# Two-layer encoder trunk: late rows squared behind evictions, roundings placed behind exponentials, memory keys and values loaded in place, the FFN's last unit in another order

## The chip, the cores and the metric

The kernel runs on one core of one Trainium2 chip. The time is the device time of one execution in microseconds. The core's engines are PE (TensorE, matrix products; its weight loads are shown as PEld), DVE (VectorE), ACT (ScalarE), POOL (GpSimd) and SP (SyncE, which issues transfers). Each engine runs its instructions in order; engines wait for one another through semaphores.

## The reference

Two layers over 1024 tokens of width 1024. Layer 0 mixes tokens by windowed attention (16 heads, 4 key/value heads, rotary, a sink per head), layer 1 by a bidirectional gated recurrence (HGRN2). Each mixer also has four heads that attend to 256 memory tokens, and each layer ends in a gated channel mixer with a short convolution. Cut to what matters:

```python
for layer in range(DEPTH):
    u = rmsnorm(h, norm_g[layer, 0])
    mem_kv = mem_n @ w_mem_kv[layer]
    y = mixer_window_attn(u, mem_kv, ...) if layer == 0 else mixer_hgrn2(u, mem_kv, ...)
    h = h + rmsnorm(y, norm_g[layer, 1])
    f = conv_ffn(rmsnorm(h, norm_g[layer, 2]), ffn_w_in[layer], ffn_conv_w[layer], ...)
    h = h + rmsnorm(f, norm_g[layer, 3])

def mixer_window_attn(u, mem_kv, w_in, sink, w_out, pos):
    q, k, v, xq = jnp.split(u @ w_in, [...], axis=-1)
    q, k = rope(q, pos), rope(k, pos)
    o = window_gqa_sink(q, k, v, sink)
    return jnp.concatenate([o, memory_cross_attn(xq, mem_kv)], axis=-1) @ w_out

def conv_ffn(v, w_in, conv_w, conv_b, w_out):
    gate, up = jnp.split(v @ w_in, 2, axis=-1)
    return (jax.nn.gelu(dwconv_centred(gate, conv_w, conv_b)) * up) @ w_out
```

## The kernel before

An fp32 product is made of three products of rounded parts: each operand is split into a rounded part (`wh`, `uh`, ...: a cast, mostly on ACT) and the rest (`wl`, `ul`, ...: a subtraction, mostly on DVE), and `mm3` (L81 to L83) or `mmk` (L535) issues high by high, low by high and high by low. A scheduler places all instructions of the program on their engines by its own estimate of time; `tc.issue_after(ins)` makes it place what is inside behind `ins`. So the order of the work is that of the schedule, and a change of one line can move others.

The program: `start()` projects the memory tokens to keys and values for both layers, stores them in `kvd`, and brings in the input; `window()` is layer 0's mixer, `Out` its output projection, `ffn` its channel mixer; `hgrn()`, `Out` and `ffn` do the same for layer 1.

**The rows' norms in layer 0.** The input is projected without its norm. The reciprocal root of each row's mean square (`rs`) is applied later: `rooted` (L1272) makes it from the sum of squares `xss` (L1274 on DVE, L1275 on POOL) and scales cos and sin (L1277) and two more factors by it. The sums come from `square` in `start()`: a load of 128 rows of x on SP (L1336) into one of three buffers, and an ACT square with a running sum (L1337). There are eight; the last three (rows 5, 6 and 7) are called together.

**The first projection.** `proj(g)` makes queries, keys and values of head group g, token block by token block (eight blocks of 128). `token(t)` runs 24 matmuls into `pj` (two buffers), turns the queries and keys on DVE (L277, L278) and POOL (L279, L280), casts v on ACT (L282) and takes its rest on DVE (L283), which is the last reader of that `pj` buffer. `turn` transposes (`ptq`, L295) and splits again. The tiles `kh`, `kl` and `v` live in one pool for even groups and in another for odd ones.

**The cross heads.** For each of the four memory heads, `cross_head` (L182 to L187) loads its keys and values from `kvd` into a tile `kv` (L185), and splits them into `kvh` (ACT, L86) and `kvl` (DVE, L87), one buffer each. In layer 0 `kv` has a tile of its own in the pool `ea`; in layer 1 it takes one of the five `E` buffers of the recurrence, so its load waits until one is free.

**The output projection's operands.** The heads' outputs go to `oT` in memory and come back: `Out.read` (L428 to L430) loads six 128-row pieces into `ul`, casts them to `uh` on ACT (L429) and takes the rest on DVE (L430). Group 3's own outputs (pieces 6 and 7) are moved inside the core and cast in `attend` (L375, L376) right behind that transfer. `wo0.begin` (L456) reads eight column blocks in turn.

**The FFN.** Units f = 0 to 21 of hidden columns are computed with seven products each (k = 1 to 7) of sums and differences of halves. Products 6, 7 and 4 use the bank X, 5 and 3 use V, 2 uses Y. ACT copies X to `su`, `g` (two halves) and V to `s5`; DVE adds; `conv` makes the gate.

## Time and profile before

| | us |
|---|---|
| median of three runs | 2674.11 |
| the three runs | 2675.33, 2672.37, 2674.11 |
| the profiled execution's own time | 2671.58 |
| its span, first to last instruction | 2669.8 |
| DVE busy | 1822.3 |
| ACT busy | 1379.6 |
| POOL busy | 471.4 |

The span is one execution's and is 1.8 us shorter than that execution's time. A timeline row has the start, the duration, the engine, the line, the operation, output <- input, its shape, and in brackets how long its engine had idled before it and what ended that. PE's matmuls overlap, so their distance from start to start is the cost of one, not the duration. The mean granted clock of PE over the span is 0.996 of full speed.

### The profile page before, as it was taken

To read this page: it belongs to the slowest core of one execution; us is meant where nothing else is said; L and a number is where in the kernel's file an instruction comes from. 1 tells how busy PE (TensorE), PEld (TensorE's weight loads), DVE (VectorE), ACT (ScalarE), POOL (GpSimd) and SP (SyncE) were. 2 spreads that over 40 slices of the span, in tenths; PEclk is the share of its full clock that TensorE was granted. 3 is DMA by queue.
4 is the path that set the end of the run, shared out by engine and by line. 5 is a ranking of instruction groups with operands and counts; after the bars stand their busy time and mean duration, and the time that the engine had idled before them with its cause. 6 is when DMAs were issued, how large, how long until landed. Compare 5 with 4: busy or idle time off the path is not lost.

```text
span 2669.8 us, 39096 instructions
## 1 busy us (share of the span) xinstructions
PE 2606.9 (98%) x14420; PEld 2188.4 (82%) x14420; DVE 1822.3 (68%) x3043; ACT 1379.6 (52%) x2503; POOL 471.4 (18%) x519
## 2 busy tenths in 40 slices
PE   8999999999999999999999999999999999999998
PEld 7888887788888887887887888888888788888887
DVE  6688786578555565478688686886757755656447
ACT  6467677445444445455454554645534444444453
POOL 0331120211111100031224131230311111110013
PEclk9999999999999999999999999999999999999999
DMA  9682223367777857574235352113436778785666
GB/s 369 222 181 59 70 69 95 104 193 193 199 201 193 210 145 259 193 246 151 87 108 147 84 123 60 48 29 92 143 126 177 188 199 210 197 204 161 223 190 236
DMA packets 195728, 425.93 MB, mean 160 GB/s; under 512 B 20048, under 2 KB 56272, under 8 KB 189904
## 3 DMA queue, kind: packets, MB, share of 16 engines
q1 hardware_dynamic: 161840, 325.11, 37.8%
q0 software_dynamic: 24544, 90.19, 16.3%
q10 hardware_dynamic: 9152, 8.14, 1.0%
q8 instruction: 113, 1.85, 0.3%
q14 instruction: 79, 0.65, 0.1%
HBM read 330.04 MB, written 116.39 MB: 167 GB/s over the span
## 4 chain that ended last, share of the span: by engine, by line
PE 78%; DVE 12%; DMA 4%; ACT 3%; issue 2%; POOL 1%; SPq 0%; ACTq 0%; DVEq 0%; POOLq 0%
PE X L535 27%; PE V L535 11%; PE pj L81 6%; PE pj L82 5%; PE pj L83 5%; PE Y L535 5%; PE pb L81 4%; PE pb L82 4%; PE pb L83 4%; DVE E L1091 1%; PE pt L362 1%; DVE ER L1126 1%; PE po L1194 1%; DVE wl L87 1%; DVE EP L1127 1%
## 5 line engine op out<-in xcount | busy, mean ns | idle before, releaser
L87 DVE TENSOR_TENSOR wl<-st,wh 128x1024 fp32r<-128x1024 f32 (+1 forms) x238 | 263.7, 1114 | 326.5 <-ACT wh L86 308.8
L86 ACT CAST wh<-st 128x1024 fp32r<-128x1024 f32 (+1 forms) x238 | 222.5, 937 | 296.4 <-PE X L535 196.3
L81 PE MATMUL pj<-uh,wh 128*128 128x512 f32 x512 | 203.9, 399 | 5.9 <-DVE q L1036 2.7
L535 PE MATMUL X<-wl,wh 128*128 128x512 f32 x528 | 204.8, 390 | 0.2 <-DVE wl L87 0.2
L535 PE MATMUL X<-wh,wl 128*128 128x512 f32 x528 | 204.6, 389 | 0.0
L81 PE MATMUL pj<-wh,uh 128*128 128x384 f32 (+1 forms) x512 | 191.5, 375 | 11.9 <-DVE v L283 6.6
L82 PE MATMUL pj<-ul,wh 128*128 128x512 f32 x512 | 202.3, 396 | 0.1
L83 PE MATMUL pj<-uh,wl 128*128 128x512 f32 x512 | 202.0, 395 | 0.0
L535 PE MATMUL X<-wh 128*128 128x512 f32 x528 | 198.7, 390 | 1.0 <-ACT c L908 1.0
L83 PE MATMUL pj<-wh,ul 128*128 128x384 f32 (+1 forms) x512 | 187.9, 368 | 0.0
L82 PE MATMUL pj<-wl,uh 128*128 128x384 f32 (+1 forms) x512 | 187.8, 367 | 0.1
L77 DVE TENSOR_TENSOR wl<-st,wh 128x1024 fp32r<-128x1024 f32 (+1 forms) x92 | 117.4, 1280 | 26.0 <-ACT wh L76 25.2
L535 PE MATMUL V<-uh,wh 128*128 128x512 f32 x344 | 133.8, 389 | 0.0
L535 PE MATMUL V<-ul,wh 128*128 128x512 f32 x344 | 133.8, 389 | 0.0
L535 PE MATMUL V<-uh,wl 128*128 128x512 f32 x344 | 133.8, 389 | 0.0
L76 ACT CAST wh<-st 128x1024 fp32r<-128x1024 f32 (+1 forms) x98 | 98.8, 1014 | 39.7 <-PE pj L82 25.0
L81 PEld LDWEIGHTS pj<-uh,wh 128*128 128x128 f32 x512 | 96.5, 189 | 26.3 <-DVE q L1036 3.6
L535 PEld LDWEIGHTS X<-wh 128*128 128x128 f32 x528 | 99.1, 188 | 22.0 <-ACT c L908 1.4
L81 PEld LDWEIGHTS pj<-wh,uh 128*128 128x128 f32 x512 | 97.4, 190 | 23.7 <-issue 9.3
L535 PEld LDWEIGHTS X<-wl,wh 128*128 128x128 f32 x528 | 99.1, 188 | 21.3 <-DVE wl L87 0.8
L535 PEld LDWEIGHTS X<-wh,wl 128*128 128x128 f32 x528 | 99.1, 188 | 20.7
L83 PEld LDWEIGHTS pj<-uh,wl 128*128 128x128 f32 x512 | 96.7, 189 | 19.1
(390 smaller groups left out, 7169.5 us busy)
## 6 DMA issues: line engine op xcount, KB each, us to landing
st<-hid SPq DMA_DIRECT2D x154, 256.0 KB, 3.1
st<-in_ffw_dram SPq DMA_DIRECT2D x108, 256.0 KB, 2.9
w2s<-in_ffw_dram POOLq DMA_DIRECT2D x24, 1024.0 KB, 8.0
st<-in_ffw_dram SPq DMA_DIRECT2D x46, 512.0 KB, 4.4
hid<-tt SPq DMA_DIRECT2D x88, 256.0 KB, 4.8
st<-w2s SPq DMA_DIRECT2D x88, 256.0 KB, 3.4
sx<-in_ffw_dram SPq DMA_DIRECT2D x84, 256.0 KB, 3.9
sy<-in_ffw_dram SPq DMA_DIRECT2D x42, 512.0 KB, 6.2
```

Of the source, the lines that this page charges most:

```text
L76: act.copy(h[:, :n], raw)
L77: (eng or dve).tensor_tensor(l[:, :n], raw, h[:, :n].bitcast(F32), op=ALU.subtract)
L81: pe.matmul(o, ah, bh, start=first, stop=False)
L82: pe.matmul(o, ah, bl, start=False, stop=False)
L83: pe.matmul(o, al, bh, start=False, stop=last)
L86: act.copy(h, src)
L87: dve.tensor_tensor(l, src, h.bitcast(F32), op=ALU.subtract)
L362: pe.transpose(tp[:, j, :], sm[:, j, c * P:(c + 1) * P], ident)
L535: pe.matmul(o, x, y, start=new, stop=e, skip_group_check=not first)
L1091: dve.tensor_tensor_scan(B[:, rev], smask, a_[:, rev], 0.0, op0=ALU.mult, op1=ALU.add)
L1126: dve.tensor_tensor(re_, re_, bc(pl_[:, :, e:e + 1], [P, nb, n]), op=ALU.mult)
L1127: dve.tensor_tensor(pl_, pl_, bc(pe_[:, :, e:e + 1], [P, nb, n]), op=ALU.mult)
```

## The change

Four parts.

- The sums of squares of rows 5, 6 and 7 leave `start()`. In `proj(0)`, behind the v cast of tokens 0, 1 and 2, `token(t)` loads row block t + 5 into a tile `row` that has the memory of `kh`, `kl` and `v` of the odd groups, which are not in use yet, and squares it there.
- `cross_head` loads the keys and values straight into `kvl`, casts `kvh` from it and subtracts in place. The tile `kv` of layer 0 and the `E` buffer of layer 1 are no longer taken. The load now has to wait for the last reader of the previous head's `kvl`.
- The casts and subtractions of group 3's pieces 6 and 7 are made by `split_moved`, behind the exponentials of an even block that follows (the last right away), and the casts of `Out.read` for column blocks 6 and 7 are placed behind the exponentials of group 3's block 1.
- The last unit of each FFN has a body of its own, `last_unit`, with the products written in the order 6, 2, 7, 5, 4, 3; before: 2, 5, 6, 7, 3, 4.

```diff
@@ -179,9 +179,10 @@
                 nc.sync.dma_start(kvd[l][:, :, 1, t * P:(t + 1) * P].rearrange("h p d -> p h d"),
                                   vm[:, t, :].rearrange("p (h d) -> p h d", h=4))
 
-    def cross_head(l, h, wp, raw):
+    def cross_head(l, h, wp):
         kvh = wp.tile([P, 2, 256], F32R, tag="kvh", bufs=1, name="kvh")
         kvl = wp.tile([P, 2, 256], F32R, tag="kvl", bufs=1, name="kvl")
+        raw = kvl.bitcast(F32)
         nc.sync.dma_start(raw, kvd[l][h])
         split(kvh, kvl, raw)
         return *wunit(A["wxq"][l, h]), kvh, kvl
@@ -279,7 +280,14 @@
                 pool.tensor_tensor(rq[:, :320], t1, t2, op=ALU.add)
                 done = pool.tensor_tensor(rq[:, 320:], t1[:, 256:], t2[:, 256:], op=ALU.add)
                 sum_steps[0].send(done)
-                act.activation(v[:, t, :64], ps[:, 320:], AF.Copy, scale=rs0[:, t:t + 1])
+                cast = act.activation(v[:, t, :64], ps[:, 320:], AF.Copy, scale=rs0[:, t:t + 1])
+                if g == 0 and t + 5 < NT:
+                    tag = ("kh", "kl", "v")[t]
+                    row = ap_.tile([P, NT, P] if tag == "v" else [P, T], F32R, tag=tag, bufs=1, name="row").bitcast(F32)
+                    row = row.rearrange("p a b -> p (a b)") if tag == "v" else row
+                    nc.sync.dma_start(row, A["x"][(t + 5) * P:(t + 6) * P, :])
+                    with tc.issue_after(cast.ins):
+                        act.activation(row, row, AF.Square, accum_out=xss[:, t + 5:t + 6])
                 dve.scalar_tensor_tensor(v[:, t, 64:], ps[:, 320:], rs0[:, t:t + 1], v[:, t, :64].bitcast(F32),
                                          op0=ALU.mult, op1=ALU.subtract)
                 return rq
@@ -317,6 +325,14 @@
             return kept
 
         pairs, roped = {}, {}
+
+        marks, moved = {}, []
+
+        def split_moved():
+            ts_ = moved.pop()
+            oh, ol = uh[:, 6:8, ts_], ul[:, 6:8, ts_]
+            act.copy(oh, ol.bitcast(F32))
+            dve.tensor_tensor(ol, ol.bitcast(F32), oh.bitcast(F32), op=ALU.subtract)
 
         def attend(g, qkv, blocks=range(NT)):
             qs, kh, kl, v = qkv
@@ -346,8 +362,11 @@
                     dve.tensor_tensor(st["es"], sk[:, 4 * g:4 * g + 4], st["nm"], op=ALU.add)
                     act.activation(st["es"], st["es"], AF.Exp)
                     for j in range(4):
-                        act.activation(sm[:, j, :w], sm[:, j, :w], AF.Exp, bias=st["nm"][:, j:j + 1], scale=0.125,
-                                       accum_out=st["su"][:, j:j + 1])
+                        marks[g, n] = act.activation(sm[:, j, :w], sm[:, j, :w], AF.Exp, bias=st["nm"][:, j:j + 1],
+                                                     scale=0.125, accum_out=st["su"][:, j:j + 1])
+                    if moved and n % 2 == 0:
+                        with tc.issue_after(marks[g, n].ins):
+                            split_moved()
                     dve.tensor_tensor(st["su"], st["su"], st["es"], op=ALU.add)
                     dve.reciprocal(st["rd"], st["su"])
                     for j in range(4):
@@ -369,11 +388,11 @@
                     dve.tensor_tensor(ov, po[:64], ov, op=ALU.add)
                     if nn % 2 == 1 and g == 3:
                         ts_ = slice((n - 1) * P, (n + 1) * P)
-                        oh, ol = uh[:, 6:8, ts_], ul[:, 6:8, ts_]
+                        moved.append(ts_)
                         for hp in range(2):
                             nc.sync.dma_start(ul[hp * 64:(hp + 1) * 64, 6:8, ts_].bitcast(F32), o[:, hp::2, :])
-                        act.copy(oh, ol.bitcast(F32))
-                        dve.tensor_tensor(ol, ol.bitcast(F32), oh.bitcast(F32), op=ALU.subtract)
+                        if n == NT - 1:
+                            split_moved()
                     elif nn % 2 == 1:
                         ts_ = slice((n - 1) * P, (n + 1) * P)
                         for hp in range(2):
@@ -385,7 +404,7 @@
                 for _ in range(XU[g][b]):
                     xh_, xb_ = units.pop(0)
                     if xb_ == 0:
-                        xhead[0] = cross_head(0, xh_, ea, ea.tile([P, 2, 256], F32, tag="kv", bufs=1, name="kv"))
+                        xhead[0] = cross_head(0, xh_, ea)
                     cross_unit(0, xh_, xb_, xhead[0], ap_, tags, ea, pair)
 
         dve.tensor_scalar_mul(sk8, sk, 8.0)
@@ -398,7 +417,7 @@
         attend(3, cur)
         wo0.open()
         y0 = wo0.w1.tile([P, NT, 512], F32, bufs=1, name="y0")
-        wo0.begin(psq, ("pj", "pj", "ptq"), [y0[:, t, :] for t in range(NT)])
+        wo0.begin(psq, ("pj", "pj", "ptq"), [y0[:, t, :] for t in range(NT)], {6: marks[3, 1], 7: marks[3, 1]})
         psp.release()
         ap_.release()
 
@@ -422,11 +441,12 @@
                     self.us[b, u] = wunit(A[self.key][b, u], pl=pl if i >= RING else None)
             self.b = b
 
-        def read(self, ks, c0, c1, eng):
+        def read(self, ks, c0, c1, eng, behind=None):
             c = (slice(None), slice(ks[0], ks[-1] + 1), slice(c0, c1))
             raw = ul[c].bitcast(F32)
             eng.dma_start(raw, oT[self.l][ks[0]:ks[-1] + 1, :, c0:c1].rearrange("k p t -> p k t"))
-            act.copy(uh[c], raw)
+            with tc.issue_after(behind.ins) if behind else nullcontext():
+                act.copy(uh[c], raw)
             dve.tensor_tensor(ul[c], raw, uh[c].bitcast(F32), op=ALU.subtract)
 
         def kept(self, ps, t, ks, first, last):
@@ -447,7 +467,7 @@
                 c = slice((k % 2) * 512, (k % 2 + 1) * 512)
                 mm3(ps, oh[:, i, :], ol[:, i, :], wh[:, c], wl[:, c], first and i == 0, last and i == 3)
 
-        def begin(self, psb, tags, y0):
+        def begin(self, psb, tags, y0, behind={}):
             self.psb, self.y0 = psb, y0
             self.banks += [(psb, t, tags.count(t)) for t in tags]
             eng = (nc.sync, act)[self.l]
@@ -456,7 +476,7 @@
                     with tc.high_priority(AHEAD):
                         self.read(self.groups[0], t * P, (t + 1) * P, eng)
                 else:
-                    self.read(self.groups[0], t * P, (t + 1) * P, eng)
+                    self.read(self.groups[0], t * P, (t + 1) * P, eng, behind.get(t))
                 ps = self.bank()
                 self.kept(ps, t, self.groups[0], True, True)
                 act.copy(y0[t], ps)
@@ -687,6 +707,30 @@
             dve.tensor_tensor(t2[:, hi], t2[:, lo], c[:, oi], op=ALU.subtract)
             for k, x in ((5, t1[:, lo]), (7, t1[:, hi]), (6, t2[:, lo]), (4, t2[:, hi])):
                 nc.sync.dma_start(hd[k, p], x)
+
+        def last_unit(w, x, v, y, s1, ahead):
+            u = fp.tile([P, T], F32, tag="u", bufs=1, name="u")
+            su = fp.tile([P, 512], F32, tag="su", bufs=1, name="su")
+            s5 = fp.tile([P, 512], F32, tag="s5", bufs=1, name="s5")
+            g = gtile()
+            prod(6, w(6), x, False)
+            act.copy(su, x)
+            prod(2, w(2), y, True)
+            dve.tensor_tensor(u[:, ti], y, s1, op=ALU.add)
+            ahead()
+            prod(7, w(7), x, False)
+            act.copy(g[:, tj], x)
+            prod(5, w(5), v, True)
+            act.copy(s5, v)
+            dve.tensor_tensor(g[:, tj], g[:, tj], s5, op=ALU.add)
+            ahead()
+            prod(4, w(4), x, False)
+            act.copy(g[:, ti], x)
+            ahead()
+            prod(3, w(3), v, False)
+            dve.tensor_tensor(u[:, tj], v, su, op=ALU.add)
+            ahead()
+            hidden(NF - 1, conv(NF - 1, g, u))
 
         def first_units():
             X, s, ops = [], {}, []
@@ -770,6 +814,10 @@
                 x = X.pop()
                 v, y = (psx.tile([P, 512], F32, tag=t, name=t) for t in "VY")
                 w = lambda k: operand(ops, k)
+                if f == NF - 1:
+                    last_unit(w, x, v, y, s[1], ahead)
+                    yield
+                    return
                 prod(2, w(2), y, True)
                 u = fp.tile([P, T], F32, tag="u", bufs=1, name="u")
                 dve.tensor_tensor(u[:, ti], y, s[1], op=ALU.add)
@@ -1223,8 +1271,7 @@
                 xh_, xb_ = units.pop(0)
                 if xhead[1] != xh_:
                     xhead[1] = xh_
-                    raw = early.tile([P, 512], F32, tag="E", bufs=5, name="kv")
-                    xhead[0] = cross_head(1, xh_, wp, raw.rearrange("p (a b) -> p a b", a=2))
+                    xhead[0] = cross_head(1, xh_, wp)
                 cross_unit(1, xh_, xb_, xhead[0], wp, tags, wp, pair)
 
         def head(h, r):
@@ -1359,8 +1406,7 @@
 
         parts = iter([(), (), (memory_rstd,)] + [(lambda k=k: part(k),) for k in range(KT - 1)]
                      + [(lambda: part(KT - 1), lambda: square(A["x"], 0, xss))]
-                     + [(lambda t=t: square(A["x"], t, xss),) for t in (1, 2, 3, 4)]
-                     + [tuple(lambda t=t: square(A["x"], t, xss) for t in (5, 6, 7))])
+                     + [(lambda t=t: square(A["x"], t, xss),) for t in (1, 2, 3, 4)])
 
         def step():
             for f in next(parts, ()):
```

How the schedule's rows move, at three places. First ACT, where `start()` ends and the first projection begins; before:

```order
L76 CAST wh<-st 128x768
L1337 ACTIVATE x,xss<-x 128x1024 x4
L282 ACTIVATE v<-pj,rs_86 128x64
L86 CAST kvh<-kv 128x512
L282 ACTIVATE v<-pj,rs_86 128x64 x3
L303 CAST qs<-ptq 64x512
L282 ACTIVATE v<-pj,rs_86 128x64
L86 CAST kh<-ptq 128x512
L305 CAST qs<-ptq 64x512
L303 CAST qs<-ptq 64x512
L305 CAST qs<-ptq 64x512
L282 ACTIVATE v<-pj,rs_86 128x64 x2
```

and with the change:

```order
L76 CAST wh<-st 128x768
L1384 ACTIVATE x,xss<-x 128x1024
L283 ACTIVATE v<-pj,rs_86 128x64 x2
L290 ACTIVATE row,xss<-row 128x1024 x2
L86 CAST kvh<-kvl 128x512
L283 ACTIVATE v<-pj,rs_86 128x64
L290 ACTIVATE row,xss<-row 128x1024
L283 ACTIVATE v<-pj,rs_86 128x64 x2
L311 CAST qs<-ptq 64x512
L86 CAST kh<-ptq 128x512
L313 CAST qs<-ptq 64x512
L311 CAST qs<-ptq 64x512
```

The squares of L1337 are those of `start()` (now L1384), L282 (now L283) is the v cast, `row` the moved square. Three of the squares stood ahead of token 0's v cast; they now stand behind the casts of tokens 1 and 2, and the kvh cast stands between them.

Second ACT in layer 1, around the kvh cast of the third memory head; before:

```order
L1099 ACTIVATE ER<-E 128x512
L1111 ACTIVATE E<-E 128x16x16
L1112 ACTIVATE E<-E 128x16x16
L998 ACTIVATE gs<-pj 128x2x128
L999 ACTIVATE gs<-gs 128x2x128
L1000 ACTIVATE gs<-gs 128x2x128
L86 CAST kvh<-kv 128x512
L1084 ACTIVATE E<-s 128x512
L998 ACTIVATE gs<-pj 128x2x128
L999 ACTIVATE gs<-gs 128x2x128
L1000 ACTIVATE gs<-gs 128x2x128
L1085 ACTIVATE E<-E 128x512
```

and with the change:

```order
L1160 ACTIVATE E<-E 128x16x16
L86 CAST ph<-pt 128x512
L100 ACTIVATE junk,oss<-po 128x128 x4
L1132 ACTIVATE E<-s 128x512
L76 CAST wh<-st 128x1024
L231 COPY xo<-pu 128x512
L232 DMA oT_58<-xo 128x512
L86 CAST kvh<-kvl 128x512
L1260 ACTIVATE ot<-pt,bng 128x512
L1133 ACTIVATE E<-E 128x512
L1134 ACTIVATE E<-E,lb 128x512
L1136 ACTIVATE s<-s,lno 128x512
```

L998 to L1000 (`gs`, now L1046 to L1048) are a sigmoid's steps in three instructions, L1084 to L1086 (now L1132 to L1134) those of the forget gate; L230 (now L231) copies a memory head's output. The cast stood behind sigmoid steps; it now stands right behind the copy of the previous head's last output.

Third ACT at the last unit of the first FFN; before:

```order
L779 COPY s_9365<-V 128x512
L86 CAST wh<-st 128x1024
L794 COPY g<-X 128x512
L564 ACTIVATE c<-g,cb,ncw 128x1024
L782 COPY su<-X 128x512
L86 CAST wh<-st 128x1024
L567 ACTIVATE c<-c 128x1024
L86 CAST wh<-st 128x1024
L785 COPY g<-X 128x512
L86 CAST wh<-st 128x1024
L794 COPY g<-X 128x512
L564 ACTIVATE c<-g,cb,ncw 128x1024
```

and with the change:

```order
L724 COPY s_9330<-V 128x512
L86 CAST wh<-st 128x1024
L842 COPY g<-X 128x512
L584 ACTIVATE c<-g,cb,ncw 128x1024
L717 COPY su<-X 128x512
L86 CAST wh<-st 128x1024
L587 ACTIVATE c<-c 128x1024
L86 CAST wh<-st 128x1024
L722 COPY g<-X 128x512
L86 CAST wh<-st 128x1024
L728 COPY g<-X 128x512
L584 ACTIVATE c<-g,cb,ncw 128x1024
```

`su`, `s` and `g` are the copies out of PE's banks X and V, L564 and L567 (now L584 and L587) the convolution and the gate, L86 casts of weights. Nothing moved here; the lines have other numbers.

## The prediction

> **What bounds the kernel now.** I read the page's sums first. The first line is the span of the profiled execution, the second each engine's busy time and share.
>
> ```profile
> span 2669.8 us, 39096 instructions
> ...
> PE 2606.9 (98%) x14420; PEld 2188.4 (82%) x14420; DVE 1822.3 (68%) x3043; ACT 1379.6 (52%) x2503; POOL 471.4 (18%) x519
> ```
>
> PE computes 98% of the span. The change leaves its products alone, so a gain comes only out of its 2669.8 - 2606.9 = 62.9 us of idleness and out of matmuls that run slowly behind a pause. The view of PE's waits (sum, times, longest) says whom it waits for:
>
> ```profile
> PE pb L81 <- ACT mh L1297: 7.4, 1, 7.4
> PE pj L81 <- DVE v L283: 6.6, 3, 6.0
> PE pj L81 <- DVE gs L1022: 5.3, 5, 2.6
> ...
> PE X L535 <- ACT g L785: 2.8, 2, 1.4
> ```
>
> The first is the program's start, which is untouched. The second, one wait of 6.0 us, is where part A works; the third holds a wait of 2.6 us that belongs to B; the fourth is what D names. A pause also leaves a slow clock, which the windows (busy us of PE, PEld, DVE, ACT, POOL, then PE's clock, DMA share, GB/s) show behind those two:
>
> ```profile
> 70.00:74.00 4.00, 3.63 (x11) 3.66 (x12) 0.40 (x2) 0.00 (x0) 0.00 (x0) 0.50 0.48 152
> ...
> 1454.00:1458.00 4.00, 3.30 (x8) 2.65 (x9) 3.74 (x5) 2.06 (x4) 1.63 (x1) 0.57 1.05 203
> ```
>
> **A, the late rows' squares.** The timeline of the first projection, all engines in time order (start, duration, in brackets the idle time before and its releaser):
>
> ```profile
> 62.16 0.38 SPq L1336 DMA_DIRECT2D x<-in_x_dram  x1
> ...
> 63.96 0.48 DVE L278 TENSOR_TENSOR t<-pj,sin 128x320 f32<-128x320 f32 x1
> ...
> 66.45 0.58 POOL L1275 TENSOR_TENSOR rs<-xss,nhalf 128x1 f32<-128x1 f32 x1
> ...
> 68.56 1.06 ACT L1337 ACTIVATE x<-x 128x1024 f32<-128x1024 f32 x1 [1.78 <-DMA x<-in_x_dram]
> ...
> 69.73 0.33 SPq L243 DMA_DIRECT2D wmask<-in_wmask_dram  x1
> ...
> 69.94 0.28 DVE L283 SCALAR_TENSOR_TENSOR v<-pj,rs,v 128x64 fp32r<-128x64 f32 x1 [5.44 <-ACT v L282]
> ...
> 70.37 0.66 PE L81 MATMUL pj<-wh,uh 128*128 128x384 f32 x1 [5.98 <-DVE v L283]
> ...
> 74.20 0.62 ACT L86 CAST kvh<-kv 128x512 fp32r<-128x512 f32 x1 [4.29 <-DMA kv<-kvd]
> ...
> 74.85 0.69 DVE L87 TENSOR_TENSOR kvl<-kv,kvh 128x512 fp32r<-128x512 f32 x1 [1.17 <-ACT kvh L86]
> 75.46 0.24 DVE L1277 TENSOR_SCALAR cos<-cos,rs 128x32 f32<-128x32 f32 x1
> ...
> 76.99 0.49 PE L295 MATMUL ptq<-ident,rq 128*128 128x128 f32 x3
> 77.24 0.28 DVE L283 SCALAR_TENSOR_TENSOR v<-pj,rs,v 128x64 fp32r<-128x64 f32 x1 [0.41 <-ACT v L282]
> 77.67 0.41 PE L81 MATMUL pj<-wh,uh 128*128 128x384 f32 x1 [0.19 <-DVE v L283]
> ...
> 81.93 0.49 PE L295 MATMUL ptq<-ident,rq 128*128 128x128 f32 x3
> 82.18 0.42 PE L81 MATMUL pj<-wh,uh 128*128 128x384 f32 x1
> ```
>
> Two pj buffers exist, so token 2's matmuls (70.37) wait until token 0's bank has been read by its v subtraction (69.94). That stands behind the v cast on ACT, which stood in order behind the last square (68.56), which waited for a load issued at 62.16. The change's order has no square ahead of the cast. The chain then runs from DVE at 63.96: 0.48 for the product, some 0.1 until the cast has read (it waits for nothing else), 0.28 for the subtraction, 0.15 from there to PE as at 70.37: token 2 can start at 64.95, not 70.37, and after some 0.6 us of pause in place of 5.98 I take the clock as full.
>
> What is late next? At full clock a token's 24 matmuls take 81.93 - 77.67 = 4.26 us (token 2's took 6.62, 70.37 to 76.99), so token 2 runs to 69.21. Token 3 needs token 1's v: POOL's rs ends at 67.03, and the DVE work from cos to the end of that subtraction took 77.52 - 75.46 = 2.06, so 69.1; no wait. It ends at 73.5. Token 4 needs token 2's v, which on ACT now stands behind two squares and the kvh cast. SP no longer waits for a slot before wmask (62.16 now; 69.73 before): then sk (1 us) and three rows of 0.38 each, kv from 64.7. The landing times of the two loads (tile kv, then the x rows):
>
> ```profile
> DMA to landing us min/median/max: 2.6/2.9/9.3
> ...
> DMA to landing us min/median/max: 4.5/6.2/9.1
> ```
>
> Rows 5 and 6, issued at 63.5 and 63.9, land by 70.1, so their squares end near 72.1; kv has landed by then behind 1.5 MB of rows; cast 0.62, v cast 0.3, subtractions 0.69 and 0.28: token 2's v is ready near 73.8, and PE, with six transposes (2 x 0.25) to place, starts token 4 near 74.3 where it started at 82.18. **A: -7.9.** If kv takes 9.3 (landing 74.0, token 4 at 75.7), the gain is 6.5, and a slow clock behind that pause would take 1.6 more: -4.9; with nothing late, 73.97: -8.2. The three squares of 1.06 cost ACT the same either way; their rows are wanted only from token 5 on.
>
> **B, the memory keys and values in place.** In the second layer's third cross head (the timeline):
>
> ```profile
> 1450.92 0.62 ACT L86 CAST kvh<-kv 128x512 fp32r<-128x512 f32 x1 [7.26 <-DMA kv<-kvd]
> ...
> 1451.48 0.39 PE L81 MATMUL pj<-wh,uh 128*128 128x512 f32 x1
> ...
> 1451.70 0.40 PE L82 MATMUL pj<-wl,uh 128*128 128x512 f32 x1
> ...
> 1454.70 0.76 PE L81 MATMUL pj<-wh,uh 128*128 128x512 f32 x1 [2.60 <-DVE gs L1022]
> ...
> 1458.10 0.40 PE L83 MATMUL pj<-wh,ul 128*128 128x512 f32 x1
> ```
>
> ACT stood 7.26 us at the kvh cast for a load; queued behind were the sigmoid steps whose gs PE waited for. PE lost 3.00 - 0.23 = 2.77 there and, in eight matmuls at 0.425 instead of 0.23, 1.57 more: 4.3. The change's order has this cast some 46 rows of ACT earlier, so nothing stands at 1443 to 1451 any more. [...]
>
> At the cast's new place the earliest issue is the last read of the previous head's kvl, since the load overwrites it:
>
> ```profile
> 1371.86 0.40 PE L83 MATMUL pu<-ph,kvl 128*128 128x512 f32 x1
> ...
> 1375.82 0.69 ACT L1212 ACTIVATE ot<-pt,bng 128x512 f32<-128x512 f32 x1 [2.46 <-DMA oT<-xo]
> ...
> 1376.90 0.33 SPq L75 DMA_DIRECT2D st<-in_wxq_dram  x1
> ...
> 1543.18 0.69 ACT L1212 ACTIVATE ot<-pt,bng 128x512 f32<-128x512 f32 x1 [4.19 <-DMA oT<-xo]
> ```
>
> Issue at 1372.3, landing after the median 2.9 at 1375.2: ACT idles 2.46 there now and 4.19 at the next head, which hides it. At the worst 9.3 the work behind comes about 6 us late; at 1450.92 a delay of 7.26 cost PE 2.60, so up to 4.7 are free. SP stands in the load's wait with the xq weights and the ot stores behind; the first of these is issued only at 1376.9 as it is. The slot that kv took among five E tiles is also free. **B: -4.3**, bounds 0 (one new stall of the same size) and -7 (the other 5.3 - 2.6 = 2.7 us of PE's waits on gs go as well). In the first layer the load of head 3 has 10 us:
>
> ```profile
> 354.37 0.40 PE L83 MATMUL po<-ph,kvl 128*128 128x512 f32 x1
> ...
> 364.41 0.36 PE L81 MATMUL ps<-kvh,xh 128*128 128x256 f32 x1
> ```
>
> Load at most 9.3 but at the median 2.9, then 0.62 and 0.69: ready near 359, so nothing.
>
> **C, the moved roundings.** The timeline at the first of them, and a window behind it:
>
> ```profile
> 403.74 0.84 ACT L429 CAST uh<-ul 128x768 fp32r<-128x768 f32 x1 [2.74 <-DMA ul<-oT]
> ```
>
> ```profile
> 409.00:421.00 12.00, 8.22 (x37) 5.37 (x38) 10.91 (x37) 10.87 (x28) 0.00 (x0) 0.97 0.28 87
> ```
>
> ACT's 2.74 of waiting goes, and block 1's exponentials start up to two DVE subtractions earlier. But the two casts and subtractions now fall into the stretch from 409, where PE idles 12 - 8.22 = 3.8 us because DVE and ACT are full. From below, all 3.8 go; from above, two casts of 0.84 delay the kh cast that now follows them (+1.7). Nearer to the crowded row: **C: -1**.
>
> **The rest of the first layer's order** also shifts, since the scheduler fills PE anew: stretches of 16 and more matmuls without a projection product, counted in the orders, hold 595 rows instead of 517, 15% more. Such products are what PE has to do while ACT and DVE work. The window of that stage:
>
> ```profile
> 100.00:500.00 400.00, 382.73 (x2102) 331.71 (x2101) 310.70 (x812) 274.21 (x680) 61.17 (x73) 0.99 0.39 104
> ```
>
> PE idles 17.3; 15% more is **+2.6**. Bounds: -2.6, were the count no guide, and twice as much, +5.2.
>
> **D, the FFN's last unit.**
>
> ```profile
> 1002.09 0.50 PE L535 MATMUL X<-u4h,wh 128*128 128x512 f32 x1 [1.40 <-ACT g L785]
> ```
>
> In the order every engine's row stays where it was and only line numbers differ; products 7 and 4 still follow each other on X. **D: 0.**
>
> **Sum.** -7.9 - 4.3 - 1 + 2.6 = -10.6 against this execution's own 2671.58: 2661.0. The runs' median, 2674.11, is 2.5 above that execution, so I forecast **2663.5**.
>
> **Rivals.** (1) More goes than I count: C reaches -3.8, B -7, and the fill costs nothing: -7.9 - 7 - 3.8 = -18.7, so 2655.4. For it speaks that PE waits on gs in four more places; against it, the full window 409 to 421. (2) The stall moves: token 4 waits for a late kv (-4.9), the fill costs 5.2 and C 1.7, so B's 4.3 is all that is kept over: -2.3, 2671.8, no change. For it speaks the landing time of 9.3. (3) Slower: the load in place cannot be issued ahead of the last read, so in-order ACT stands at kvh at every head's change as it did at 1450.92, at 4.3 a time. With three such places in the second layer and one in the first, B is 4 x 4.3 - 4.3 = +12.9; with the other terms (-7.9 - 1 + 2.6) the sum is +6.6, so 2680.7. It decides from the fourth place on, if loads land over 4.7 us after ACT gets there. Against it: the median of 2.9, and ACT's own idleness at those places. (4) D acts after all, both waits of 1.40 go: 2660.7.
>
> **Chances.** Forecast 0.57, (1) 0.16, (2) 0.14, (3) 0.10, (4) 0.03. Within 0.2%, about what these runs can tell from no change, is 5.3 us. Faster 0.57 + 0.16 + 0.03 = 0.76, same 0.14, slower 0.10. The forecast's own bounds are 2657 to 2668; reaching to (1) and (2) gives 2654 to 2672, which leaves out (3), 0.10, and some of the outer edges.
>
> **What would show it.** Right: no wait near 5 us behind the first two tokens, token 4's first matmul near 74; no wait over 1 us of PE on gs near 1450; ACT's kvh waits under 4 us; the two 1.4 us waits on g kept. Wrong: a clock under 1 between 66 and 78, kvh waits over 5 us with PE idle behind, or an idle sum between 100 and 500 far from 19 us.

## The result, and the profile after

The changed kernel takes 2668.36 us (median of 13 runs, 2665.82 to 2673.73), the kernel before 2675.07 on the same chip (13 runs, 2670.59 to 2677.01): a ratio of 0.9981 [0.9974, 0.9989], 5.1 us less. The ratio and its 95% interval are those of the record; they are not the quotient of the two medians, which would give 0.9975 or 6.7 us. Below, "us against before" is always (ratio - 1) x 2672, so it can differ by a us or two from a difference of medians. The direction was right. The time lies in the wider range (2654 to 2672) and just outside the forecast's own bounds (2657 to 2668). The gain is 0.48 of the 10.6 forecast.

The page of the changed kernel, the lines that answer to those shown of before:

```profile
span 2666.4 us, 39108 instructions
...
PE 2601.3 (98%) x14420; PEld 2185.9 (82%) x14420; DVE 1813.5 (68%) x3043; ACT 1378.9 (52%) x2503; POOL 473.7 (18%) x519
```

PE's idleness is 2666.4 - 2601.3 = 65.1 us; it was 62.9. So in this trace the gain is not idleness taken away but matmuls that run less slowly (busy time 2606.9 to 2601.3, mean granted clock 0.996 to 0.998). In a second trace of the changed kernel (e9 below) the span is 2668.2 us and the clock 0.996, as before. The view of PE's waits (sum, times, longest) shows what replaced what:

```profile
PE pj L81 <- DVE cos L1324: 5.3, 1, 5.3
...
PE ps L355 <- ACT kh L86: 3.2, 2, 2.6
PE pt L1213 <- ACT ot L1260: 3.1, 2, 2.0
PE X L555 <- ACT g L722: 2.8, 2, 1.4
...
PE pj L81 <- DVE gs L1070: 2.5, 4, 0.8
```

Token 2's wait of 6.0 is gone and one of 5.3 stands in the same projection. The gs wait of 2.6 is gone, as forecast; an ot wait of 2.0 is new. The kh wait, 0.7 before, is 2.6. The two g waits of 1.4 are as they were.

**Part A.** The timeline of the first projection, all engines:

```profile
61.59 0.42 SPq L244 DMA_DIRECT2D wmask<-in_wmask_dram  x1
...
62.53 1.38 SPq L288 DMA_DIRECT2D row<-in_x_dram  x3
...
64.02 0.51 SPq L186 DMA_DIRECT2D kvl<-kvd  x1
64.06 0.32 ACT L283 ACTIVATE v<-pj,rs 128x64 fp32r<-128x64 f32 x1 [2.82 <-DVE xss L1321]
...
64.84 0.41 PE L81 MATMUL pj<-wh,uh 128*128 128x384 f32 x1 [0.95 <-DVE v L291]
...
65.17 0.77 POOL L138 DMA_DIRECT2D w2s<-in_ffw_dram  x1
...
69.45 0.62 POOL L138 DMA_DIRECT2D w2s<-in_ffw_dram  x1
...
78.05 0.62 ACT L86 CAST kvh<-kvl 128x512 fp32r<-128x512 f32 x1 [6.55 <-DMA kvl<-kvd]
78.57 0.31 ACT L283 ACTIVATE v<-pj,rs 128x64 fp32r<-128x64 f32 x1
...
79.31 0.28 DVE L291 SCALAR_TENSOR_TENSOR v<-pj,rs,v 128x64 fp32r<-128x64 f32 x1
...
79.73 0.66 PE L81 MATMUL pj<-wh,uh 128*128 128x384 f32 x1 [5.33 <-DVE cos L1324]
```

Token 2 starts at 64.84, where 64.95 was forecast. Part of that agreement is luck: DVE's product ahead of it began at 63.46 and not at 63.96, and the v subtraction came 0.47 behind that product's end and not 0.1. Token 4 should have followed near 74.3; PE does fall idle at 79.73 - 5.33 = 74.40, but goes on only at 79.73. The row names cos as releaser, because that was DVE's last instruction by then; what PE needs is v, written 0.14 before, and the chain behind v is read upward: v's subtraction, v's cast on ACT, and ahead of that cast in ACT's order the kvh cast, which stood 6.55 us for the load of the first memory head. The view of that tile has the landing time:

```profile
DMA to landing us min/median/max: 14.0/14.0/14.0
```

Issued at 64.02, landed at 78.02, behind three rows of 512 KB and beside POOL's loads of w2s. Of these, POOL issued three by 73.20 (two of 1 MB, the third of 768 KB). Before, its second came only at 78.01, since POOL waited 9.89 us for DVE; that kernel's timeline of POOL:

```profile
76.92 0.86 POOL L279 TENSOR_TENSOR rq<-t,t 128x320 f32<-128x320 f32 x1 [9.89 <-DVE xss L1274]
...
78.01 0.62 POOL L138 DMA_DIRECT2D w2s<-in_ffw_dram  x1
```

So taking away token 2's stall also brought the second w2s load forward, from 78.01 to 69.45, into the time in which the memory head's load was under way. Behind the stall the windows (busy us of PE, PEld, DVE, ACT, POOL, PE's clock, DMA share, GB/s) show the clock down:

```profile
74.00:78.00 4.00, 0.40 (x4) 0.16 (x2) 0.00 (x0) 0.00 (x0) 0.40 (x1) 1.00 0.95 348
78.00:82.00 4.00, 2.27 (x7) 2.30 (x8) 2.46 (x10) 2.18 (x5) 1.11 (x3) 0.71 0.12 49
82.00:86.00 4.00, 4.00 (x21) 4.00 (x21) 0.83 (x5) 0.00 (x0) 1.15 (x3) 0.87 0.69 240
```

DMA stands at 0.95 while every engine waits for a 256 KB transfer. So token 4 starts 82.18 - 79.73 = 2.45 us earlier than before, and not the 7.9 forecast.

**Part C.** The timeline at the roundings' new place:

```profile
413.61 1.55 ACT L449 CAST uh<-ul 128x768 fp32r<-128x768 f32 x2
...
415.18 0.59 ACT L86 CAST kh<-ptq 128x512 fp32r<-128x512 f32 x1
...
415.82 1.01 PE L355 MATMUL ps<-kh,qs 128*128 128x384 f32 x2 [2.60 <-ACT kh L86]
```

Both roundings stand back to back ahead of the kh cast, and PE waits 2.60 for kh. Before, its row had 0.68:

```profile
418.91 0.61 PE L339 MATMUL ps<-kh,qs 128*128 128x384 f32 x2 [0.68 <-ACT kh L86]
```

Two windows behind the wait of 2.60 have the clock at half:

```profile
416.00:418.00 2.00, 1.89 (x5) 1.38 (x6) 2.00 (x4) 2.00 (x3) 0.00 (x0) 0.50 0.00 0
418.00:420.00 2.00, 2.00 (x6) 1.52 (x6) 2.00 (x5) 2.00 (x8) 0.00 (x0) 0.50 0.35 76
```

The slow clock is not new there. A window of before has 0.66, and one of the changed kernel without part C (e8 below) has 0.50:

```profile
419.00:423.00 4.00, 3.41 (x10) 2.61 (x11) 4.00 (x13) 4.00 (x8) 0.00 (x0) 0.66 0.09 9
```

```profile
416.00:420.00 4.00, 3.29 (x9) 2.17 (x8) 3.29 (x12) 3.98 (x8) 0.00 (x0) 0.50 0.02 4
```

**Part B.** The old stall's stretch, then ACT and PE one head later:

```profile
1454.00:1458.00 4.00, 4.00 (x20) 3.30 (x19) 3.67 (x9) 1.88 (x4) 0.08 (x1) 1.00 1.02 211
```

```profile
1533.62 0.33 SPq L186 DMA_DIRECT2D kvl<-kvd  x1
...
1540.31 0.62 ACT L86 CAST kvh<-kvl 128x512 fp32r<-128x512 f32 x1 [5.62 <-DMA kvl<-kvd]
1540.83 0.68 ACT L1260 ACTIVATE ot<-pt,bng 128x512 f32<-128x512 f32 x1
1541.41 0.62 ACT L1133 ACTIVATE E<-E 128x512 f32<-128x512 f32 x1
1541.56 0.65 PE L1213 MATMUL pt<-ident,ER 128*128 128x128 f32 x4 [1.96 <-ACT ot L1260]
```

The clock is 1.00 where it was 0.57, PE never idle. But one head later the load, which cannot be issued before the last read of kvl, landed 6.7 us after its issue; ACT stood at kvh and ot came late.

### The profile page after: what moved, and what is told of

It is laid out like the page before. It is cut to its first block, busy times and chain, and to the rows that moved or that the text cites. A ratio compares the mean times of both kernels' runs of the same rounds, so it can differ in the third digit from the quotient of the medians.

```text
span 2666.4 us, 39108 instructions
## 1 busy us (share of the span) xinstructions
PE 2601.3 (98%) x14420; PEld 2185.9 (82%) x14420; DVE 1813.5 (68%) x3043; ACT 1378.9 (52%) x2503; POOL 473.7 (18%) x519
## 4 chain that ended last, share of the span: by engine, by line
PE 79%; DVE 12%; DMA 3%; ACT 3%; issue 1%; POOL 1%; SPq 0%; ACTq 0%; DVEq 0%; POOLq 0%
PE X L555 28%; PE V L555 11%; PE pj L81 6%; PE pj L82 5%; PE pj L83 5%; PE Y L555 5%; PE pb L81 4%; PE pb L83 3%; PE pb L82 3%; DVE E L1139 1%; PE pt L381 1%; DVE wl L77 1%; DVE ER L1174 1%; DMA kvl<-kvd 1%; PE po L1242 1%
## 5 line engine op out<-in xcount | busy, mean ns | idle before, releaser
L86 ACT CAST wh<-st 128x1024 fp32r<-128x1024 f32 (+1 forms) x238 | 222.5, 937 | 293.8 <-PE X L555 196.2
L925 POOL TENSOR_TENSOR c<-c,g 128x512 f32<-128x512 f32 x24 | 43.8, 1844 | 392.4 <-PE X L555 163.0
```

The lines of the kernel that those rows point to most:

```text
L86: act.copy(h, src)
L925: pool.tensor_tensor(y[q][:, t, :], y[q][:, t, :], g3[:, c], op=ALU.mult)
```

## The experiments

One marker separates the layers: the row of the first FFN's last product that waits 1.4 us for g, here of the changed kernel (start, duration, wait).

```profile
1000.54 0.50 PE L555 MATMUL X<-u4h,wh 128*128 128x512 f32 x1 [1.39 <-ACT g L722]
```

Before it stood at 1002.09. Every run: its median, and its ratio to runs of before on the same chip; the marker is of the one traced execution (D forced has no such row):

| run | kernel | median us | ratio [95%] | us | marker |
|---|---|---|---|---|---|
| | changed | 2668.36 | 0.9981 [0.9974, 0.9989] | -5.1 | 1000.54 |
| e1 | changed, first head's load first | 2664.83 | 0.9970 [0.9959, 0.9981] | -8.0 | 993.97 |
| e2 | changed without A | 2673.74 | 1.0006 [0.9997, 1.0014] | +1.6 | 1001.87 |
| e3 | changed, kvh behind ot | 2674.96 | 1.0009 [1.0000, 1.0017] | +2.4 | 1001.04 |
| e4 | changed, D forced | 2665.69 | 0.9974 [0.9965, 0.9983] | -6.9 | - |
| e5 | changed, w2s loads later | 2661.79 | 0.9955 [0.9941, 0.9969] | -12.0 | 994.34 |
| e6 | e1 and e4 | 2658.64 | 0.9947 [0.9934, 0.9959] | -14.2 | - |
| e7 | B alone | 2675.09 | 1.0011 [1.0002, 1.0020] | +2.9 | 1004.75 |
| e8 | changed without C | 2665.20 | 0.9972 [0.9964, 0.9981] | -7.5 | 999.70 |
| e9 | changed, traced again | 2667.21 | 0.9981 [0.9972, 0.9990] | -5.1 | 999.80 |
| e10 | A alone | 2670.21 | 0.9985 [0.9975, 0.9994] | -4.0 | 1000.64 |
| e11 | e6 without C | 2660.82 | 0.9962 [0.9949, 0.9975] | -10.2 | - |
| e12 | e11 and e5 | 2659.38 | 0.9953 [0.9940, 0.9966] | -12.6 | - |
| e13 | B alone, layer 1 | 2669.43 | 0.9992 [0.9983, 1.0001] | -2.1 | 1002.53 |
| e14 | B alone, layer 0 | 2676.99 | 1.0015 [1.0007, 1.0024] | +4.0 | 1002.95 |
| e15 | C alone | 2674.82 | 1.0008 [0.9999, 1.0016] | +2.1 | 1000.84 |
| e16 | A alone, load first | 2667.66 | 0.9983 [0.9975, 0.9992] | -4.5 | 995.18 |
| e17 | changed, B in layer 1 only | 2670.12 | 0.9991 [0.9982, 1.0000] | -2.4 | 1003.57 |
| e18 | e16, B in layer 1, D forced | 2660.10 | 0.9959 [0.9947, 0.9972] | -11.0 | - |

An interval is 2 to 4 us to each side, so two rows are told apart from about 3 to 5 us on. Single executions of one kernel scatter by up to 13 us (e1: 2658.72 to 2672.06).

The traces of some runs can be compared stage by stage, because PE goes through the same sequence of matmuls in them. In the first layer these groups share one sequence up to the marker, and their markers lie within 0.4 to 1.8 us: before and e13 (1002.09, 1002.53); changed, e9 and e3 (1000.54, 999.80, 1001.04); e7 and e14 (1004.75, 1002.95). In the second layer, from the marker to the same row of the second FFN, the scatter is larger. With the loads as before it took 1447.1, 1451.2, 1447.2, 1453.9 and 1451.4 us (before, e10, e14, e15, e16), with the loads in place 1443.8 to 1449.2 (changed, e1, e2, e5, e7, e8, e9, e13, e17). So one trace says little of a part worth 3 us in the second layer. The means of the two groups, 1450.1 and 1446.0, differ by 4.1.

### The late load: e1, e5, e2

**e1** issues the first head's load ahead of the mask, the sink and the rows (`cross_load` is the part of `cross_head` that makes the tile and loads it).

```diff
+        kv0 = [cross_load(0, 0, ea)]
         nc.sync.dma_start(wmask, A["wmask"])
...
-                        xhead[0] = cross_head(0, xh_, ea)
+                        xhead[0] = cross_head(0, xh_, ea, kv0.pop() if kv0 else None)
```

> The changed kernel, with the first memory head's load of keys and values issued ahead of the mask, the sinks and the three late rows. Theory: the 5.33 us wait of token 4 (79.73 in the changed kernel) comes from this load, which took 14.0 us behind the rows and two 1 MB loads of POOL's queue, and held the kvh cast and token 2's v cast behind it. Then token 4 starts near 74.3, its matmuls run at full clock, and the kernel gains 5.4 + 1.2 = 6.6 us on the changed one: about 11.7 under before. Rival: the late rows hold ACT in the same place themselves (the third landed at 73.55); then token 4 still waits some 3 us or more and the gain is under 3 us.

Its timeline, then its windows where the changed kernel stood:

```profile
61.96 0.43 SPq L184 DMA_DIRECT2D kvl<-kvd  x1
...
65.76 0.62 ACT L86 CAST kvh<-kvl 128x512 fp32r<-128x512 f32 x1 [1.02 <-DMA kvl<-kvd]
...
72.65 0.31 ACT L287 ACTIVATE v<-pj,rs 128x64 fp32r<-128x64 f32 x1
```

```profile
74.00:78.00 4.00, 4.00 (x26) 3.97 (x24) 1.66 (x8) 1.47 (x3) 2.54 (x5) 1.00 0.95 377
78.00:82.00 4.00, 4.00 (x26) 3.92 (x26) 2.68 (x10) 1.85 (x5) 2.52 (x6) 1.00 0.75 279
```

The load lands 3.7 us after its issue, v of token 2 is cast at 72.65 instead of 78.57, and PE is full at full clock through both windows. The marker comes 6.2 earlier than the changed kernel's mean of two traces (1000.17), close to the 6.6 expected. By the ratios e1 gains only 2.9 on the changed kernel, with about 3 us of uncertainty: the mechanism is shown by the trace, its price by the ratio is smaller than the marker says.

**e5** leaves the load where it is and begins POOL's w2s loads three tokens later.

```diff
-                sum_steps[0].send(done)
+                if g or t > 2:
+                    sum_steps[0].send(done)
```

> The changed kernel with POOL's first 1 MB loads of w2 begun three tokens later; the load of the first head's keys and values still stands behind the three late rows. It tells who made that load take 14.0 us. If the two 1 MB loads did, it lands in 6 to 8 us (the 1.5 MB of rows at the 348 GB/s of that stretch are 4.4 us), token 4 does not wait, and the kernel gains 4 to 6.6 us on the changed one. If the rows alone did, it still takes over 10 us. The schedule of the attention behind it also shifts, which blurs the total by a few us either way.

The view of its kvl tile, then its timeline:

```profile
DMA to landing us min/median/max: 8.0/8.0/8.0
```

```profile
71.58 0.30 ACT L284 ACTIVATE v<-pj,rs 128x64 fp32r<-128x64 f32 x1
...
72.85 0.60 ACT L86 CAST kvh<-kvl 128x512 fp32r<-128x512 f32 x1
...
76.20 0.77 POOL L138 DMA_DIRECT2D w2s<-in_ffw_dram  x1
```

Without POOL's transfers beside it the load takes 8.0 instead of 14.0, in the same SP order; the first w2s now goes out at 76.20. So the load landed at 64.39 + 8.0 = 72.4: the three rows alone do not bring it past the 74.0 that the forecast allowed. The scheduler also put v ahead of kvh, so not all of the gain is the landing's. The marker is 994.34, 5.8 earlier than the changed kernel's mean, and the time -12.0. The run delays all of POOL's early loads at once, so it does not tell the first from the second.

**e2** puts the squares of rows 5 to 7 back at the start (B, C, D stay).

```diff
-                    with tc.issue_after(cast.ins):
-                        act.activation(row, row, AF.Square, accum_out=xss[:, t + 5:t + 6])
...
+                     + [tuple(lambda t=t: square(A["x"], t, xss) for t in (5, 6, 7))])
```

> The changed kernel with the squares of rows 5 to 7 back in the start. Theory: part A as made was worth 0.6 to 2 us only, since its stall came back at token 4; so this stands 3 to 4.5 us under before, with the 6 us wait of token 2 back. Rival: A brought its 7.9 and something else in the changed kernel lost 5; then this kernel is 2 to 3 us slower than before.

The theory missed, and the time is near the rival's: +1.6 [-0.8, +3.7]. Without A nothing is gained, so B, C and D together are worth +1.6 and not the forecast's -4.3 - 1 + 2.6 + 0 = -2.7.

### B in the second layer: e3, e13, e7

**e3** places layer 1's kvh cast behind the latest ot activation, so that ot cannot stand behind a late load.

```diff
-        split(kvh, kvl, raw)
+        with tc.issue_after(last_ot[0].ins) if l and last_ot else nullcontext():
+            split(kvh, kvl, raw)
...
-            act.activation(ot, tp, AF.Identity, scale=bng[:, h:h + 1])
+            last_ot[0] = act.activation(ot, tp, AF.Identity, scale=bng[:, h:h + 1])
```

> The changed kernel with the cast and the subtraction of a memory head in the second layer placed behind the latest output activation (ot). Theory: the 1.96 us wait of PE on ot near 1541 comes from ACT standing 5.62 us at the kvh cast for a load of 6.67 us; behind ot nothing of the recurrence's output waits for it, and the kernel gains about 2.2 us on the changed one, 7.3 under before, with no wait over 1 us on gs near 1450. Rival: the wait is that of ot for its own buffer (the row of before names a transfer out of xo, 4.19 us), and nothing is gained there.

A miss: +2.4. The cast moved some 60 us later (the last from 1703.1 to 1766.6) and waits for nothing there. But in its waits `PE pa L1170 <- POOL E L1185: 6.7, 5, 1.6` is up from 2.6, and PE waits 2.49 on ot at 1550.10. That ot waited for the transfer out of its own buffer (2.09 us on ACT), as the rival had it. Moving the cast moved the stall.

**e13** is before with only the second layer in place (the diff); layer 0's order is that of before. **e7** has the change's B in both layers and neither A, C nor D.

```diff
+        raw = kvl.bitcast(F32) if raw is None else raw
         nc.sync.dma_start(raw, kvd[l][h])
...
-                    raw = early.tile([P, 512], F32, tag="E", bufs=5, name="kv")
-                    xhead[0] = cross_head(1, xh_, wp, raw.rearrange("p (a b) -> p a b", a=2))
+                    xhead[0] = cross_head(1, xh_, wp, None)
```

> The kernel before with the loads in place in the second layer alone; the order of the first layer is that of before. If the stall at 1454 is a loss of 4.3 that nothing takes over, this is 2 to 4.3 us under before. If the recurrence passes it on (waits on ot near 1541 and on q near 1560 and 1720, as in the trace of B alone, where the second layer gained only 0.3), it is within 1.5 us of before.

> The kernel before with part B alone (memory keys and values loaded in place, no E buffer taken). Theory: the 2.60 us wait and the slow clock at 1454 go, 4.3, and 0.6 to 2 come back as a wait on ot near 1541, since ACT stands at the kvh cast there; so 2 to 3.5 us under before. Rival: nothing is left of it, within 1 us of before, because the recurrence passes the slack on to its next wait (on q near 1560).

e13: -2.1 [-4.5, +0.3], an interval that holds both theories. Its second layer took 1443.8 us, before's 1447.1. Its waits lose the gs wait of 2.6; its row one head later is milder than the changed kernel's:

```profile
1541.55 0.66 PE L1166 MATMUL pt<-ident,ER 128*128 128x128 f32 x4 [0.80 <-ACT ot L1213]
```

What is given back differs from trace to trace: PE's wait there is 1.96 in the changed kernel, behind a load that landed 6.7 us after its issue, 0.84 in e9 and 0.80 in e13. e7, a miss too, has no gs wait over 0.8 either, yet is 2.9 slower. Its second layer took as long as before's (1447.1) and its marker is 2.7 later, which points to the first layer.

### B in the first layer and C: e14, e17, e15, e8

**e14** is before with only the first layer in place, **e17** the changed kernel with only the second. The diff is e14's, beside the line in `cross_head` that e13 has.

```diff
-                        xhead[0] = cross_head(0, xh_, ea, ea.tile([P, 2, 256], F32, tag="kv", bufs=1, name="kv"))
+                        xhead[0] = cross_head(0, xh_, ea, None)
```

> The kernel before with the loads in place in the first layer alone. In the trace of B alone the first layer lost 2.8 us, most of it in waits of PE on the rows' maxima and on the kh cast between 410 and 425. If that is the cause, this is 2 to 3.5 us slower than before with those two waits; if the second layer made B's loss, it is within 1 us of before.

> The changed kernel with the first layer's memory heads loaded into a tile of their own again (in place only in the second layer); the late load behind the rows stays. Theory 1, the missing half of the gain is the stall at token 4 alone: token 4 still waits 3.6 to 5.3 us, the first layer's marker (the last product 4 of its FFN) stays near 1000.5, the time is that of the changed kernel within 1.5 us, ratio to before 0.998. Theory 2, loading in place in the first layer costs inside the change what it cost alone (+4.0): the marker comes near 997 and the ratio is 0.9966, with the same wait at token 4.

e14 is 4.0 slower by the ratio. Its trace has both waits in the pinch, as I call the crowded stretch at 410 to 422, where before had no wait over 1.02:

```profile
411.92 0.44 PE L340 MATMUL ps<-kh,qs 128*128 128x384 f32 x1 [2.23 <-DVE mx L343]
...
420.82 1.01 PE L340 MATMUL ps<-kh,qs 128*128 128x384 f32 x2 [1.98 <-ACT kh L86]
```

Its marker, though, is only 0.9 later than before's (e7's, in the same sequence, 2.7), so the trace does not show where all of the 4.0 goes. And taking the loads in place out of the changed kernel's first layer (e17) does not give 4 us back. It comes out 2.7 slower than the changed kernel (-2.4 against -5.1; the two intervals overlap), with the marker 3 us later. Here the packing leaves another hole in the same place:

```profile
418.89 1.09 PE L303 MATMUL ptq<-ident,rq 128*128 128x128 f32 x4 [4.56 <-DVE qs L314]
```

So "in place costs 4 in the first layer", theory 2 of that run, falls. Theory 1 had the wait at token 4 (3.95 us here) but not the time. The likely cause is how the scheduler happens to pack this pinch, which every part changes; no run holds that packing still.

**e15** is C alone, **e8** the changed kernel without C. The diff is e8's; it also takes the marks out of the call of `wo0.begin`.

```diff
-                        moved.append(ts_)
+                        oh, ol = uh[:, 6:8, ts_], ul[:, 6:8, ts_]
...
-                        if n == NT - 1:
-                            split_moved()
+                        act.copy(oh, ol.bitcast(F32))
+                        dve.tensor_tensor(ol, ol.bitcast(F32), oh.bitcast(F32), op=ALU.subtract)
```

> The kernel before with part C alone. By my forecast 1 us under before; by the changed kernel (2.3 slower with C than without) 1 to 3 us slower, with a wait of over 2 us on the kh cast near 416; if C matters only through the order that the other parts make, within 1 us.

> The changed kernel with the roundings of part C back in their places. My forecast gave C -1, so this would be 1 us slower than the changed one, 4 under before. Against it stands the changed kernel's own wait of 2.60 us on the kh cast at 415.8, which was 0.68 before: if the moved casts made it, this kernel is 1 to 2 us faster than the changed one, 6 to 7 under before, and that wait is back under 1 us.

By the ratios C costs about 2: +2.1 [-0.3, +4.3] alone, 2.4 by the difference of the changed kernel and e8, whose intervals overlap. e15 has the wait that was expected of it:

```profile
417.95 0.61 PE L347 MATMUL ps<-kh,qs 128*128 128x384 f32 x2 [2.90 <-ACT kh L86]
```

In e8 the roundings are back (its timeline), and kh comes in time:

```profile
401.76 0.83 ACT L449 CAST uh<-ul 128x768 fp32r<-128x768 f32 x1 [1.04 <-DMA ul<-oT]
...
416.68 0.59 ACT L86 CAST kh<-ptq 128x512 fp32r<-128x512 f32 x1
...
417.31 1.01 PE L355 MATMUL ps<-kh,qs 128*128 128x384 f32 x2 [0.60 <-ACT kh L86]
```

So in the changed kernel the kh wait comes with C and goes with it. It is not C's alone: e14, without C, has one of 1.98. e8 has, besides, a wait of 1.81 at 408.00 that the changed kernel has not. C works ahead of the marker, and there the traces show no cost of 2: e15's marker is 1.3 earlier than before's, and e8's (999.70) only 0.8 earlier than the mean of the three traces with the changed kernel's first layer (1000.46). What made e15's trace long is its second layer, 1453.9 us in a sequence of matmuls that is before's. The size of C is not settled, and its sign neither.

### D: e4

The last unit's products 7, 5, 4 and 3 are each tied behind the one before.

```diff
-            prod(4, w(4), x, False)
+            with tc.issue_after(fifth.ins):
+                fourth_ = prod(4, w(4), x, False)
```

> The changed kernel with the products 7, 5, 4 and 3 of each FFN's last unit bound to be issued in that order. Theory: the part D of the change did not reach the schedule; in the forced order product 5 covers the copy of X, both waits of 1.39 us on g go, and the kernel gains 2.8 us on the changed one, 7.9 under before. Rival: with product 3 last the hidden columns come later, the wait at the start of the second product (1.57 us on c) grows by as much, and nothing is gained.

Now the written order is the one that runs. In its timeline each layer keeps one wait of 0.68 instead of 1.39:

```profile
991.21 0.50 PE L555 MATMUL X<-u7h,wh 128*128 128x512 f32 x1 [0.68 <-ACT su L718]
...
2434.71 0.50 PE L555 MATMUL X<-u7h,wh 128*128 128x512 f32 x1 [0.68 <-ACT su L718]
```

2 x (1.39 - 0.68) = 1.4; the ratios differ by 1.9 (intervals overlap). The rival did not come: the wait on c, 1.57 in the changed kernel, is not among e4's waits. As built, D did nothing.

### A by itself, and the same kernel again: e10, e16, e9

**e10** is before with A only, **e16** the same with the first head's load ahead of the mask. **e9** is the changed kernel, its text unaltered but for an empty line.

```diff
+        kv0 = [ea.tile([P, 2, 256], F32, tag="kv", bufs=1, name="kv")]
+        nc.sync.dma_start(kv0[0], kvd[0][0])
         nc.sync.dma_start(wmask, A["wmask"])
```

> The kernel before with part A alone, the keys and values in a tile of their own as before. Two loads of them now follow the rows on SP. Theory: token 2's wait of 6 us goes and token 4's of 3.5 to 5.3 comes, as in the changed kernel; since B alone is 3.0 slower, C costs 2.3 and the changed kernel is 5.1 under before, A alone must be worth about 10 if the parts add up; by its stalls it is worth 1 to 3. If it comes out near 10 under before, the parts add up and A's gain reaches beyond its stall; if near 2, the parts do not add up, and the order that all of them make together in the attention decides.

> The kernel before with part A alone and the first head's load ahead of the rows, in a tile of its own. The forecast's term for A was 7.9, of which A alone had 4.0. If the load was all that stood in its way, this is 7 to 9 us under before and token 4 does not wait; if more of A's gain is lost in the order behind it, 4 to 6.

> The changed kernel itself, with a second trace, beside the runs below. If its stalls are made by the order, the same waits stand in the second trace: token 4's, with a landing of the first head's load of 12 us or more, and under 1 us on gs near 1450. The time: again some 5 us under before. What differs between the two traces by more than 0.5 us belongs to the single execution.

e10 stands at token 4 for 3.6 us, e9 for 3.85 (landing 12.5), e17 for 3.95 (12.8), the first trace for 5.33 (14.0): the stall is there in every kernel with A as built and POOL's loads in their places, and in the three traces with a landing beside it its length follows the landing. e16 has no such stall, and its marker is 5.5 ahead of e10's. Yet the ratios of e10 and e16 lie only 0.5 apart, -4.0 and -4.5: e10 is between its two expectations, e16 in its second. By the traces e10's and e16's second layers take 1451.2 and 1451.4 us (before 1447.1, in the same sequence), so neither says why e16's ratio shows so little; this stays open.

### Together: e6, e11, e12, e18

e6 is e1's and e4's edits; e11 leaves out C; e12 adds e5's later loads to e11; e18 is e16's early load, B in the second layer only and D forced.

```diff
+        kv0 = [cross_load(0, 0, ea)]
         nc.sync.dma_start(wmask, A["wmask"])
...
+            with tc.issue_after(seventh.ins):
+                fifth = prod(5, w(5), v, True)
```

> The first memory head's load ahead of the rows and the last unit's products in the forced order, together. The two work in different places (near 80, and near 1000 and 2446), so the gains add up: 8.0 of the one and 2.8 of the other, 10 to 11 us under before, ratio near 0.996. Rival: the wait at the start of the second product (2.28 us in the first of them) grows by what the last unit gains; then 8.

> The first head's load ahead of the rows, the last unit's products in the forced order, and part C's roundings back in their places. The kernel without C gained 2.3 on the changed one; if that adds up with the 14.1 of the first two, 16 us under before, ratio near 0.994. Rival: C costs only in the order of the changed kernel and matters nothing here: 14.

> As the run before, with POOL's first 1 MB loads three tokens later too. With the first head's load already ahead of the rows nothing waits for it; the later loads only let the rows land sooner, which nothing waits for either. So within 3 us of the run before, either way, from the other order of the attention.

> Before, with the late squares and the first memory head's load ahead of the mask (as in the run with A and the early load), in place in the second layer only, the FFN's last products forced into the written order, the roundings where they were. Theory 1, the parts add as their own runs measured: -4.5 - 2.1 - 1.9 = -8.5, ratio 0.9968; by the trace's -7.1 in the first layer -11.1, ratio 0.9958. Theory 2, in place in the first layer costs 4.0 wherever it stands: 4.0 less than the run with the early load, in place in both layers, D forced and no moved roundings (-10.2), so -14.2, ratio 0.9947, as good as the best version so far.

e6 has the lowest median, 2658.64 us, 0.9947 [0.9934, 0.9959], 14.2 below before and faster than both kernels; 10 to 11 was expected. It is not told apart from e5, e11, e12 and e18, whose intervals overlap its own. e11, without C, missed its 14 to 16: it is 4.0 slower than e6 where e8 was 2.4 faster than the changed kernel, which the intervals of e6 and e11 do not tell from nothing. In e11 the pinch has two waits (2.33 on mx, 1.99 on kh), in e6 one of 2.90. e12 lies within 3 us of e11, as expected. e18, without C and without B in the first layer, comes to -11.0 [-14.2, -7.5]. That is near theory 1's -11.1 by the trace, but theory 1's -8.5 lies in the interval as well and theory 2's -14.2 on its edge, so e18 decides little.

## Why the prediction was right in direction and half in size

**A, -7.9: the step that failed is "kv has landed by then behind 1.5 MB of rows".** The first half held to 0.1 us (token 2 at 64.84 for 64.95), in part by errors that cancel, and behind the pause of 0.95 the clock was 1.00 from 66 to 74, as the forecast took it. The landing did not: 78.0, where at most 74.0 (9.3 us) was allowed. The 9.3 came from the same tile's worst load before, but none of those went out behind three 512 KB rows with loads of 1 MB and 768 KB of another queue beside them. The rows were in the forecast; POOL's loads were not, though the change itself let the second one go at 69.45 instead of 78.01. e5's one trace shows what that was worth: behind the same rows, without POOL's loads, the landing took 8.0, within the 9.3, and came at 72.4, close to the 72.1 at which the forecast wanted it. With the four parts kept and the lateness gone, the time is -8.0 (e1) and -12.0 (e5), on either side of the forecast's -10.6; the attention's order differs in both. By the markers the late load is worth 6.2 and 5.8. So the missing 5.5 is chiefly this term, with 2.9 (e1) and 6.9 (e5) as its size by the ratios. Rival (2) had the mechanism, a stall moved to token 4 by a late kv, with too short a landing. Of the signs named for a wrong forecast this one came: kvh waits over 5 us, 6.55 and 5.62, with PE idle behind.

**C, -1.** The upper bound's mechanism, two casts ahead of the kh cast, is what happened (kh wait 0.68 to 2.60). Its price is open: about +2 by the ratios, whose intervals do not settle it, and between -1.3 and +0.8 by the markers. If the ratios are right, up to 3 more of the missing 5.5 are here.

**B, -4.3.** The stall at 1454 is gone with B in the second layer (no wait on gs over 0.8 in the changed kernel, e1 to e9, e11, e13, e17 and e18), and in the changed kernel its slow clock is gone too (1.00 for 0.57). That half the sum came back one head later was not forecast: "up to 4.7 are free" was read from the delay at 1450.92, but here ACT's delay of 5.62 cost PE 1.96, on ot and not on gs. Alone the second layer gave -2.1 [-4.5, +0.3], inside the bounds of 0 and -7. The mean second layer of all traces is 4.1 shorter with the loads in place, near the 4.3, with a scatter of 5 to 7 us in either group. So no run shows that this term is what is missing.

**Packing, +2.6, and C together** were to raise PE's idleness between 100 and 500 by 1.6, to 19; it rose to 18.6 (from 17.3). The sum was right. The split over parts was not to be had from counts, as e14 and e17 with their opposite signs show, and no run tests the 15% by itself.

**D, 0:** right, for the reason given: the scheduler issued products 7 and 4 behind each other as before, and only forcing the order (e4) moved the waits.

**Rival (3),** ACT held at every head's change at 4.3 a time, did not come. The changed kernel's view of the kvl tile has ACT's waits for it over both layers:

```profile
  DMA kvl<-kvd: 16.1, 4
```

Four waits, of which 6.55 is A's and 5.62 the one at 1540; the other two make 16.1 - 6.55 - 5.62 = 3.9 together, and no wait of PE over 1 us stands behind them.

**What stays open.** By the ratios the parts alone (A -4.0, B +2.9, C +2.1) make +1.0, the whole -5.1. Three intervals of 2 to 3 us to each side can explain much of it, the packing of the pinch near 415, which every part alters, perhaps some more; the runs do not separate the two, nor do they explain e16's ratio.
